# Half of a modulation sum moved to ScalarE and GpSimd, first down-projection copies to ScalarE, and two orderings changed in a one-core encoder step

## The chip, the cores and the metric

The kernel runs on 1 core of one Trainium2 chip. The metric is the device time of one execution in microseconds; lower is better. A core has a matrix engine (PE, TensorE), a vector engine (DVE, VectorE), an activation engine (ACT, ScalarE), a general engine (POOL, GpSimd) and a queue that issues DMAs (SP, SyncE). Each of them executes its own list of instructions strictly in order; an instruction whose semaphore is not yet set holds up everything behind it on that engine.

## The reference

One step of a one-layer streaming encoder over 1024 prompt frames and 32 sample frames, model width 1024, in f32:

```
mod = silu(c) @ w_mod + b_mod            # c: one row for the prompt, one for the sample
sh1, sc1, g1, sh2, sc2, g2, sh3, sc3, g3 = split(mod, 9)
h = rmsnorm(x, gains[0]) * (1 + sc1) + sh1
x = x + 0.5 * g1 * rmsnorm(swiglu(h, w1_gate, w1_up, w1_down), gains[1])     # block 1
h = rmsnorm(x, gains[2]) * (1 + sc2) + sh2
x = x + g2 * rmsnorm([GN(mixer A) ; GN(mixer B)] @ w_out, gains[3])          # mixers
h = rmsnorm(x, gains[4]) * (1 + sc3) + sh3
x = x + 0.5 * g3 * rmsnorm(swiglu(h, w2_gate, w2_up, w2_down), gains[5])     # block 2
swiglu(h, wg, wu, wd) = (silu(h @ wg) * (h @ wu)) @ wd                       # inner width 2816
```

`w_mod` is 1024 x 9216. Its product with the two rows of silu(c), one for the prompt and one for the sample, is what the code calls modulation.

## The kernel before

The 1056 frames are three token blocks `tb` = 0, 1, 2 of 384, 384 and 288 columns (the last holds the 32 sample frames); the features lie on the 128 partitions. Every f32 product is made from three matmuls: activation and weight are each split into a high part and a remainder, and high x high, high x low and low x high are summed in PSUM. A weight tile is split by `pair_of` (lines 539 and 540): ACT copies the high part, then DVE, or POOL for a sum of weights, subtracts to get the rest.

**The two feed-forward blocks** (`ffn`, key "h1" for block 1 and "h3" for block 2) run over 11 groups of 256 inner columns. A round is three stages: "g" (gate), "u" (up) and "d" (down). Gate and up of token blocks 0 and 1 are one Strassen-Winograd product (`strassen`): seven 12-matmul products instead of eight, from weights A11, A12, A21, A22 and their sums S1 to S4, which POOL adds (`Mat.of`, line 563) and splits (line 540), and from activation sums T1 to T4 (`combos`, lines 614 to 632). Token block 2 shares the weights A11 to A22. Round 0 uses no sums (`plain`), because T1 to T4 need the normed activations of both token blocks; its up weights lie in three places of a tile called `wu`. Before each product the code asks for the split of its own weight and of the next product's. In the down stage (`down`, lines 796 to 803) two PSUM banks `dn` fill; the first group of a token block copies them to the accumulator `facc` (line 801, DVE), later groups add them (line 803, DVE). `facc` of the attention output is called `fo`.

**Side work.** Norms, residuals, modulation and the sums T are Python generators in a list `side`; `step(n)` advances the first of them by n pieces, and calls of `step` stand between products. `begin` appends a generator (or puts it first), and `need(key)` runs the list until the one with that key is done. `between(F, tb, ...)` is residual and norm of one token block; its sums of squares go through a matmul with a column of ones (`pss`, line 374), a reciprocal root (`ry`, lines 351 to 355) and a broadcast (`pr`, line 422).

**Modulation.** The first 16 of 72 column blocks are made at the start by matmuls. The other 56 come as side work in block 1 (`mod_aside`, 19 chunks of up to 384 columns): a DMA brings 256 rows of `w_mod` into a tile `wma`, and for each of the eight 128-row slices DVE multiplies it by the silu column of the prompt (j = 0) and adds it to `macc` 0, and does the same for the sample (j = 1, `macc` 1): lines 248 (first slice) and 250. Then three transposes and a DVE reduction per row sum over the partitions (lines 256 and 257).

`wma`, the weight sums `ws` and the norms' scratch tiles share one pool of five buffers, "h". The order on each engine is not written by hand: a scheduler that lists the program's pieces by their place in the code, and by when it expects their inputs, sets it when the program is built. So a moved `begin` or a new request changes the lists of all engines.

Of the kernel before, what the change touches and what calls it, by code (L numbers as in the profile page):

```python
# [10 lines left out]
AF = mybir.ActivationFunctionType  # L11
OP = mybir.AluOpType
AX = mybir.AxisListType
# [68 lines left out]
def encoder_step(ctx: ExitStack, tc, x_prompt, x_sample, cache_a_k, cache_a_v, cache_b_k, cache_b_v,  # L82
# [152 lines left out]
    def mod_aside(c0, nc_):  # L235

        w = 128 * nc_
        acc = [s_tile([128, 384], "macc")[:, :w] for _ in range(2)]
        for g in range(4):
            r = h_tile([128, 2, 384], "wma")[:, :, :w]  # L240
            dma.dma_start(r, w_mod[0, 256 * g:256 * (g + 1), 128 * c0:128 * c0 + w]
                          .rearrange("(k p) n -> p k n", p=128))
            for kk in range(2):
                k = 2 * g + kk
                for j in range(2):
                    c = csil[:, k, j:j + 1]
                    if k == 0:
                        ve.tensor_scalar(acc[j], r[:, kk], c, None, op0=OP.mult)
                    else:
                        ve.scalar_tensor_tensor(acc[j], r[:, kk], c, acc[j], op0=OP.mult, op1=OP.add)  # L250
                yield
        yield
        for j in range(2):
            pt = pc("pmt", (128, 4, 128))
            for b in range(nc_):
                te.transpose(pt[:, b, :], acc[j][:, 128 * b:128 * b + 128], ident)
            ve.tensor_reduce(modT[:, j, c0:c0 + nc_], pt[:, :nc_, :], axis=AX.X, op=OP.add)
        coefs(c0, c0 + nc_)
        yield

# [390 lines left out]
    def ffn(key, H, tags, F, facc, wg, wu, wd, per_group, key_out, after, beside=lambda: None):  # L651
# [68 lines left out]
        def strassen(r, what, m, two, beside):  # L720
            w, w2 = 384, TB[2][1]
            B = {"B11": half(0, 0), "B21": half(0, 1), "B22": half(1, 1), **T}
            banks, v = {}, {}

            def bank(name):
                if name not in banks:
                    if name in "bd":
                        t = p2("gu")
                        banks["b"], banks["d"] = t[:, 0, :w], t[:, 1, :w]
                    elif name in "01":  # L730
                        t = p2("g2")
                        banks["0"], banks["1"] = t[:, 0, :w2], t[:, 1, :w2]
                    else:
                        banks[name] = p1("ge")[:, :w]
                return banks[name]

            def temp(name, f, tb):
                v[name] = s_tile([128, 384], "sl" if what == "g" else "ut")
                if what == "g":
                    sl[r, f, tb] = v[name]  # L740
                return v[name]

            def plus(out, b, x):
                ve.tensor_tensor(out, banks[b], v[x], op=OP.add)

            seq = [x for x in STRASSEN if two or x[1]]
            for n, (name, x, at, blk2) in enumerate(seq):
                w_ = m.split(name)
                if n + 1 < len(seq):
                    m.split(seq[n + 1][0])  # L750
                if x:
                    product(bank(at), w_, B[x], name in ("A11", "S2", "S1", "A22"), True)
                if two and blk2:
                    f, d = int(name[1]) - 1, int(name[2]) - 1
                    product(bank(str(f)), w_, half(2, d), name in ("A11", "A22"), True)
                beside(n)
                if name == "A11":
                    ae.activation(temp("s", 1, 0), banks["a"], AF.Copy)
                elif name == "A12":
                    made(r, what, 0, 0, banks["a"])  # L760
                elif name == "S2":
                    plus(temp("u", 0, 1), "b", "s")
                elif name == "S3":
                    plus(v["s"], "b", "s")
                    plus(temp("c", 1, 1), "d", "s")
                    made(r, what, 1, 1, v["c"])
                elif name == "A22":
                    plus(v["s"], "e", "s")
                    made(r, what, 1, 0, v["s"])
                elif name == "S4":  # L770
                    plus(v["u"], "d", "u")
                    made(r, what, 0, 1, v["u"])
                elif name == "A21":
                    made(r, what, 0, 2, banks["0"])
                    made(r, what, 1, 2, banks["1"])
                step(pace)
# [3 lines left out]
        def down(r, tb, m, mp):  # L780
            w = TB[tb][1]
            if mp == 0:
                owns[tb] = tb not in begun
                begun.add(tb)
                if owns[tb]:
                    F[tb] = facc(tb)
                if r == final[tb]:
                    if key_out != "y" or tb == 1:
                        finish()
                    owns[tb, "own"] = marked((key_out, tb), after(tb))  # L790
            ps = p2("dn")
            for s in range(2):
                k = 2 * mp + s
                for q in range(2):
                    g, (h, l) = gs[r, q, tb], m.w[q, k // 4]
                    te.matmul(ps[:, s, :w], h[:, k % 4, :], g[:, 0, :w], start=q == 0, stop=False)  # L796
                    te.matmul(ps[:, s, :w], h[:, k % 4, :], g[:, 1, :w], start=False, stop=False)  # L797
                    te.matmul(ps[:, s, :w], l[:, k % 4, :], g[:, 0, :w], start=False, stop=q == 1)  # L798
            o = F[tb][:, 2 * mp:2 * mp + 2, :]
            if owns[tb]:  # L800
                ve.tensor_copy(o, ps[:, :, :w])  # L801
            else:
                ve.tensor_tensor(o, ps[:, :, :w], o, op=OP.add)  # L803
            if r == final[tb]:
                next(owns[tb, "own"])
            step(1)
            if r == final[tb] and mp == KT // 2 - 1:
                side.append(owns[tb, "own"])
# [2 lines left out]
        yield  # L811
        load(1)
        yield
        for i, (r, what) in enumerate(stages):
            gi, blocks = plan[r]
            if (r, what) == (0, "u"):
                continue
            load(i)
            m = loaded[r, what]

            def nexts(n, last, i=i):
                if n == 0:
                    load(i + 1)
                elif n == last:
                    ready(i + 1)

            if what == "d":
                for q in range(2):
                    m.split(q, 0)
                order = list(blocks)  # L830
                ending = any(r == final[tb] for tb in order)
                todo = [(tb, mp) for tb in order for mp in range(4)] if ending else \
                    [(tb, mp) for h in range(2) for tb in order for mp in (2 * h, 2 * h + 1)]
                for n, (tb, mp) in enumerate(todo):
                    if n == 1:
                        for q in range(2):
                            m.split(q, 1)
                    down(r, tb, m, mp)
                    nexts(n, len(todo) - 3)
            elif r == 0:  # L840
                mu = loaded[r, "u"]
                mu.places = [(None, p) for p in wide(tags)] + [("r",)]
                for tb in blocks:
                    need((key, tb))
                    if tb == 1:
                        begin((key, "T"), combos(H, T, tags), first=key == "h3")
                    last = tb == blocks[-1]
                    plain(r, "g", m, tb, lambda n: None)
                    plain(r, "u", mu, tb, lambda n, last=last: nexts(n, 2, i + 1) if last else None)
            elif blocks == (2,):  # L850
                need((key, 2))
                plain(r, what, m, 2, lambda n: nexts(n, 2))
            else:
                need((key, "T"))
                if 2 in blocks:
                    need((key, 2))
                strassen(r, what, m, 2 in blocks, lambda n: nexts(n, 4 if what == "g" else 5))
            if what == "u" or r == 0 and what == "g":
                if 2 in blocks:
                    per_group(gi)  # L860
                if gi == NF // 2 - 1:
                    beside()
# [676 lines left out]
    while outs:  # L1539
        out_piece()  # L1540
        step(OUTSTEP)
    begin(("h3", 2), between(F2[2], 2, 1, H3))


    F3 = [None] * 3

# [80 lines left out]
```

## Time and profile before

| what | value |
|---|---|
| median of 3 runs | 2287.52 us (2286.5 to 2291.86) |
| the profiled execution | 2285.75 us, of which 2284.0 us are the span from first to last instruction |
| PE busy | 2118.2 us, 93% of the span |
| DVE, ACT, POOL busy | 1510.4 us (66%), 848.1 us (37%), 649.0 us (28%) |
| granted TensorE clock, mean | 0.969 |
| HBM traffic | 164.12 MB read, 22.86 MB written |

The profile lists instructions by source line. In its rows "x" is a count, then come the busy time in us and the mean ns of one, and after a bar the idle time of the engine in front of them with what ended it. A row of waits reads: who waited for whom, us in total, times, the longest. Block 1 runs from about 45 to 850 us, the projections and mixers to about 1470, block 2 from there to the end.

### The profile page before, as it was taken

What the parts mean: (1) busy time and instruction counts of PE and PEld (TensorE: products, weight loads), DVE (VectorE), ACT (ScalarE), POOL (GpSimd) and SP (SyncE); (2) the same over time, 40 slices, a digit from 0 to 9 for tenths busy, and PEclk for the clock granted to TensorE, in tenths of its full rate; (3) what the DMA queues carried; (4) which work ended last, traced back from release to release, by engine and by line L of the source; (5) the groups of instructions that cost most, each with busy time, mean ns of one, the idle gap of its engine ahead of it and who ended that gap; (6) DMA issues with size and microseconds to landing.
All of it is one profiled execution on the core that took longest, in us unless ns stands there. A gap on an engine that the chain in (4) does not pass through costs nothing.

```text
span 2284.0 us, 34644 instructions
## 1 busy us (share of the span) xinstructions
PE 2118.2 (93%) x13532; PEld 2003.9 (88%) x13532; DVE 1510.4 (66%) x2917; ACT 848.1 (37%) x1814; POOL 649.0 (28%) x609
## 2 busy tenths in 40 slices
PE   7888989999999998999999899967999999999998
PEld 4888989999999997889888578867999999999997
DVE  5888779888865687677544775677645455544548
ACT  4422212222223344467544673433332222332224
POOL 2333222333245212200100322335143323333311
PEclk8999999999999998999999899988999999999999
DMA  8133224333232254110210211421321111111123
GB/s 317 59 105 113 90 78 122 111 98 94 77 121 66 74 185 130 63 41 25 66 30 25 81 40 44 153 74 37 111 65 47 56 38 56 56 52 32 47 65 116
DMA packets 150842, 186.10 MB, mean 81 GB/s; under 512 B 7981, under 2 KB 134357, under 8 KB 149525
## 3 DMA queue, kind: packets, MB, share of 16 engines
q1 hardware_dynamic: 150676, 183.87, 26.0%
q8 instruction: 107, 1.75, 0.3%
q14 instruction: 59, 0.48, 0.1%
HBM read 164.12 MB, written 22.86 MB: 82 GB/s over the span
## 4 chain that ended last, share of the span: by engine, by line
PE 69%; DVE 16%; DMA 6%; POOL 4%; issue 2%; ACT 2%; SPq 0%; DVEq 0%; POOLq 0%; ACTq 0%
PE gu L598 9%; PE ge L598 8%; PE dn L796 6%; PE dn L797 6%; PE dn L798 6%; PE g L598 6%; DVE macc L250 5%; PE gate L598 3%; PE po L979 2%; POOL ws L563 2%; PE S L1018 2%; PE pq L342 2%; PE up L598 2%; DMA raw<-in_w_up_dram 2%; PE pq L344 2%
## 5 line engine op out<-in xcount | busy, mean ns | idle before, releaser
L796 PE MATMUL dn<-gg,w 128*128 128x384 f32 (+1 forms) x1008 | 333.2, 331 | 51.8 <-DVE facc L801 31.3
L540 POOL TENSOR_TENSOR w<-ws,w 128x512 fp32r<-128x512 f32 x160 | 220.9, 1388 | 550.7 <-ACT w L539 547.4
L540 DVE TENSOR_TENSOR w<-raw,w 128x512 fp32r<-128x512 f32 x298 | 240.2, 815 | 193.2 <-ACT w L539 192.3
L539 ACT ACTIVATE w<-raw 128x512 fp32r<-128x512 f32 x298 | 184.1, 629 | 474.6 <-PE dn L798 187.4
L797 PE MATMUL dn<-gg,w 128*128 128x384 f32 (+1 forms) x1008 | 327.6, 325 | 0.0
L798 PE MATMUL dn<-gg,w 128*128 128x384 f32 (+1 forms) x1008 | 327.5, 325 | 0.0
L803 DVE TENSOR_TENSOR facc<-dn,facc 128x768 f32<-128x768 f32 (+1 forms) x240 | 212.6, 887 | 156.1 <-PE dn L798 154.6
L598 PE MATMUL gu<-t,w 128*128 128x384 f32 x1440 | 264.5, 335 | 3.4 <-DVE facc L803 2.6
L598 PEld LDWEIGHTS gu<-t,w 128*128 128x128 f32 x1440 | 248.4, 188 | 4.4 <-issue 3.1
L796 PEld LDWEIGHTS dn<-gg,w 128*128 128x128 f32 x1008 | 191.7, 190 | 60.2 <-DVE facc L801 32.4
L598 PE MATMUL g<-h_hi,w 128*128 128x288 f32 x1024 | 224.1, 296 | 5.0 <-DVE w L540 2.3
L563 POOL TENSOR_TENSOR ws<-raw 128x512 f32<-128x512 f32 x80 | 116.5, 1456 | 308.3 <-DVE macc L250 109.7
L250 DVE SCALAR_TENSOR_TENSOR macc<-wma,csil,macc 128x384 f32<-128x384 f32 (+1 forms) x266 | 183.6, 728 | 17.2 <-DMA wma<-in_w_mod_dram 17.1
L797 PEld LDWEIGHTS dn<-gg,w 128*128 128x128 f32 x1008 | 191.7, 190 | 0.0
L798 PEld LDWEIGHTS dn<-gg,w 128*128 128x128 f32 x1008 | 191.3, 190 | 0.0
L598 PE MATMUL ge<-h,w 128*128 128x384 f32 x960 | 185.7, 336 | 0.4 <-ACT w L539 0.4
L598 PEld LDWEIGHTS g<-h_hi,w 128*128 128x128 f32 x1024 | 171.4, 188 | 7.8 <-DVE w L540 4.7
L539 ACT ACTIVATE w<-ws 128x512 fp32r<-128x512 f32 x160 | 99.2, 630 | 201.5 <-PE g L598 82.2
L598 PEld LDWEIGHTS ge<-h,w 128*128 128x128 f32 x960 | 166.6, 188 | 0.8 <-ACT w L539 0.6
L598 PE MATMUL g<-h_lo,w 128*128 128x288 f32 x512 | 151.2, 295 | 0.0
L698 ACT ACTIVATE gg<-sl 128x384 fp32r<-128x384 f32 (+1 forms) x132 | 61.7, 492 | 144.9 <-DVE sl L697 144.3
L598 PE MATMUL ge<-t,w 128*128 128x384 f32 x480 | 99.0, 343 | 12.5 <-DVE w L540 8.7
(294 smaller groups left out, 4374.8 us busy)
## 6 DMA issues: line engine op xcount, KB each, us to landing
raw<-in_w_gate_dram SPq DMA_DIRECT2D x54, 512.0 KB, 3.8
raw<-in_w_up_dram SPq DMA_DIRECT2D x54, 512.0 KB, 3.8
raw<-in_w_down_dram SPq DMA_DIRECT2D x54, 512.0 KB, 3.9
wma<-in_w_mod_dram SPq DMA_DIRECT2D x72, 384.0 KB, 3.4
raw<-in_w_in_dram SPq DMA_DIRECT2D x18, 512.0 KB, 4.0
raw<-in_w_out_dram SPq DMA_DIRECT2D x13, 512.0 KB, 5.2
wm<-in_w_mod_dram SPq DMA_DIRECT2D x8, 768.0 KB, 8.9
xr<-xs SPq DMA_DIRECT2D x16, 384.0 KB, 3.9
```

The source lines that it names most:

```text
L250: ve.scalar_tensor_tensor(acc[j], r[:, kk], c, acc[j], op0=OP.mult, op1=OP.add)
L342: te.matmul(ps, w[:, 0, k], hi, start=start, stop=False)
L344: te.matmul(ps, w[:, 1, k], hi, start=False, stop=stop)
L539: ae.activation(w[:, 0], src, AF.Copy)
L540: (by or ve).tensor_tensor(w[:, 1], src, w[:, 0], op=OP.subtract)
L563: (ge if name in SUMS_POOL else ve).tensor_tensor(a[name], x, y, op=op)
L598: te.matmul(ps, w[a][:, k, :], x[b][k], start=first and k == 0 and q == 0, stop=last and k == n - 1 and q == 2, skip_group_check=True)
L698: ae.activation(g[:, 0, :w], v, AF.Copy)
L796: te.matmul(ps[:, s, :w], h[:, k % 4, :], g[:, 0, :w], start=q == 0, stop=False)
L797: te.matmul(ps[:, s, :w], h[:, k % 4, :], g[:, 1, :w], start=False, stop=False)
L798: te.matmul(ps[:, s, :w], l[:, k % 4, :], g[:, 0, :w], start=False, stop=q == 1)
L803: ve.tensor_tensor(o, ps[:, :, :w], o, op=OP.add)
```

## The change

- `mod_aside`: the prompt row stays on DVE. For the sample row ACT multiplies each slice by its silu column into a new tile `wmn` of the pool "h", and POOL adds the two halves of `wmn` to each other and the sum to `macc` 1. The sums over the partitions become matmuls with a column of ones (stationary `macc`, one column moving) into a PSUM tile `pms`, and one DVE copy takes both rows out. The generator yields once more per chunk.
- `strassen`: a product asks for the splits of the next two weights instead of one.
- `down`: the first group's copy to `facc` is made by ACT instead of DVE.
- `ffn` for block 2: the sums T are put on the list right after norms of token blocks 0 and 1, and the norm of token block 2 (`between(F2[2], ...)`) behind them; before, that norm was begun first, and the sums were put in front of it when token block 1's turn came.

```
--- before.py
+++ after.py
@@ mod_aside
+            n = h_tile([128, 2, 384], "wmn")[:, :, :w]
             for kk in range(2):
                 k = 2 * g + kk
-                for j in range(2):
-                    c = csil[:, k, j:j + 1]
-                    if k == 0:
-                        ve.tensor_scalar(acc[j], r[:, kk], c, None, op0=OP.mult)
-                    else:
-                        ve.scalar_tensor_tensor(acc[j], r[:, kk], c, acc[j], op0=OP.mult, op1=OP.add)
+                if k == 0:
+                    ve.tensor_scalar(acc[0], r[:, kk], csil[:, k, 0:1], None, op0=OP.mult)
+                else:
+                    ve.scalar_tensor_tensor(acc[0], r[:, kk], csil[:, k, 0:1], acc[0], op0=OP.mult, op1=OP.add)
+                ae.activation(n[:, kk], r[:, kk], AF.Copy, scale=csil[:, k, 1:2])
+                if kk:
+                    to = acc[1] if g == 0 else n[:, 0]
+                    ge.tensor_tensor(to, n[:, 0], n[:, 1], op=OP.add)
+                    if g:
+                        ge.tensor_tensor(acc[1], acc[1], n[:, 0], op=OP.add)
                 yield
         yield
+        yield
+        pm = pc("pms")[:, :2 * nc_].rearrange("p (j b) -> p j b", j=2)
         for j in range(2):
-            pt = pc("pmt", (128, 4, 128))
             for b in range(nc_):
-                te.transpose(pt[:, b, :], acc[j][:, 128 * b:128 * b + 128], ident)
-            ve.tensor_reduce(modT[:, j, c0:c0 + nc_], pt[:, :nc_, :], axis=AX.X, op=OP.add)
+                te.matmul(pm[:, j, b:b + 1], acc[j][:, 128 * b:128 * b + 128], ones, start=j == 0 and b == 0,
+                          stop=j == 1 and b == nc_ - 1, skip_group_check=True)
+        ve.tensor_copy(modT[:, :, c0:c0 + nc_], pm)
         coefs(c0, c0 + nc_)
@@ strassen
                 w_ = m.split(name)
-                if n + 1 < len(seq):
-                    m.split(seq[n + 1][0])
+                for nx in seq[n + 1:n + 3]:
+                    m.split(nx[0])
@@ down
             if owns[tb]:
-                ve.tensor_copy(o, ps[:, :, :w])
+                ae.activation(o, ps[:, :, :w], AF.Copy)
@@ ffn
         load(1)
         yield
+        if key == "h3":
+            begin((key, "T"), combos(H, T, tags))
+            begin((key, 2), between(F2[2], 2, 1, H3))
@@ ffn, round 0
-                    if tb == 1:
-                        begin((key, "T"), combos(H, T, tags), first=key == "h3")
+                    if tb == 1 and key == "h1":
+                        begin((key, "T"), combos(H, T, tags))
@@ before block 2
-    begin(("h3", 2), between(F2[2], 2, 1, H3))
```

Line numbers of the changed kernel are 7 to 10 higher from `mod_aside` on (540 becomes 547, 563 becomes 570, 598 becomes 605).

The built programs show where instructions moved. **POOL in block 1**, early in the rounds; `ws` are the weight sums, `w` their splits. Before:

```order
L563 TENSOR_TENSOR ws<-ws,raw 128x512
L563 TENSOR_TENSOR ws<-raw,ws 128x512
L563 TENSOR_TENSOR ws<-raw 128x512
L540 TENSOR_TENSOR w<-ws,w 128x512 x3
L563 TENSOR_TENSOR ws<-raw 128x512
```

The changed kernel, in the same rounds:

```order
L253 TENSOR_TENSOR macc<-wmn 128x384
L570 TENSOR_TENSOR ws<-raw 128x512
L255 TENSOR_TENSOR macc<-macc,wmn 128x384
L570 TENSOR_TENSOR ws<-ws,raw 128x512
L547 TENSOR_TENSOR w<-ws,w 128x512
L570 TENSOR_TENSOR ws<-raw,ws 128x512
L253 TENSOR_TENSOR wmn<-wmn 128x384
L255 TENSOR_TENSOR macc<-macc,wmn 128x384
L547 TENSOR_TENSOR w<-ws,w 128x512
```

One or two modulation adds now stand in front of nearly every weight sum and split of POOL; there are 133 of them in the whole list.

**PE and DVE at the start of block 2.** PE before, from the gate product of token block 0 on:

```order
L598 MATMUL gate<-h,w 128x384 x13
L598 MATMUL up<-h,wu 128x384 x22
L422 MATMUL pr<-ident,ry 128x128 x3
L598 MATMUL up<-h,wu 128x384 x14
L598 MATMUL up<-h,w 128x384 x12
L598 MATMUL gate<-h,w 128x384 x32
```

PE of the changed kernel:

```order
L605 MATMUL gate<-h,w 128x384 x13
L429 MATMUL pr<-ident,ry 128x128 x3
L605 MATMUL up<-h,wu 128x384 x4
L605 MATMUL gate<-h,w 128x384 x18
L605 MATMUL up<-h,wu 128x384 x32
L605 MATMUL up<-h,w 128x384 x12
```

The broadcast `pr` of token block 1's norm comes before the up product instead of inside it, and of that product four matmuls stand in front of token block 1's gate. DVE before, at the same place (`sq` are sums of squares, `rv` the start of the reciprocal root):

```order
L492 TENSOR_TENSOR fo<-fo,xr 128x768 x2
L540 TENSOR_TENSOR w<-raw,w 128x512
L385 TENSOR_TENSOR sq<-sq 128x384
L540 TENSOR_TENSOR w<-raw,w 128x512 x3
L385 TENSOR_TENSOR sq<-sq 128x384
L540 TENSOR_TENSOR wu<-raw,wu 128x512
L387 TENSOR_TENSOR sq<-sq 128x384
L540 TENSOR_TENSOR wu<-raw,wu 128x512 x2
```

DVE of the changed kernel, from the norm of token block 1 on (`z` and `t_...` are the sums T):

```order
L452 SCALAR_TENSOR_TENSOR n<-fo,acoef,pr 128x384 x8
L478 SCALAR_TENSOR_TENSOR h<-n,modT,h 128x384 x6
L621 TENSOR_TENSOR z<-h 128x768 x3
L630 TENSOR_TENSOR z<-z 128x768
L633 TENSOR_TENSOR z<-z 128x768
L628 TENSOR_TENSOR t_14933<-z,t_14933 128x768
L636 TENSOR_TENSOR z<-z 128x768
L628 TENSOR_TENSOR t_14934<-z,t_14934 128x768
L639 TENSOR_TENSOR z<-z 128x768
L628 TENSOR_TENSOR t_14935<-z,t_14935 128x768
L547 TENSOR_TENSOR wu<-raw,wu 128x512
```

The splits of the up weights `wu` stood ahead of that norm; now the whole norm and most of the first half of the sums T stand ahead of them.

**The first `facc` copies of block 2.** Before, on DVE, between the sums T that follow token block 2's norm:

```order
L626 TENSOR_TENSOR z<-z 128x768
L621 TENSOR_TENSOR t_15055<-z,t_15055 128x768
L629 TENSOR_TENSOR z<-z 128x768
L621 TENSOR_TENSOR t_15056<-z,t_15056 128x768
L632 TENSOR_TENSOR z<-z 128x768
L801 COPY facc<-dn 128x768 x2
L621 TENSOR_TENSOR t_15057<-z,t_15057 128x768
```

In the changed kernel, on ACT, ahead of token block 2's norm (`h_hi`):

```order
L705 ACTIVATE gg<-sl 128x384
L808 ACTIVATE facc<-dn 128x768
L388 ACTIVATE sq<-fo 128x2x288
L808 ACTIVATE facc<-dn 128x768 x2
L546 ACTIVATE w<-raw 128x512
L808 ACTIVATE facc<-dn 128x768
L546 ACTIVATE w<-raw 128x512
L808 ACTIVATE facc<-dn 128x768
L765 ACTIVATE sl<-ge 128x384
L808 ACTIVATE facc<-dn 128x768
L476 ACTIVATE h_hi<-n,modT 128x256
```

Six of the eight copies have moved from behind that norm to ahead of it. In the rounds of block 2 after round 1 the lists of DVE, ACT and POOL are the same as before, and that of PE but for two rows, up to the last round.

## The prediction

> **What bounds the kernel now.** I read the busy time by stretches first. In its rows stand the stretch in us, its length, busy us and count of PE, PEld, DVE, ACT and POOL, the granted clock, the DMA share and GB/s: here most of block 1, the start of block 2, and block 2's steady rounds.
>
> ```profile
> 100.00:690.00 590.00, 537.22 (x3286) 524.69 (x3285) 478.17 (x787) 148.78 (x273) 194.06 (x133) 0.98 0.33 99
> 1470.00:1600.00 130.00, 95.32 (x516) 93.11 (x517) 95.11 (x180) 51.94 (x97) 51.51 (x38) 0.84 0.23 76
> 1600.00:2220.00 620.00, 611.35 (x3853) 606.42 (x3853) 312.35 (x437) 178.94 (x331) 198.84 (x143) 1.00 0.19 56
> ```
>
> Block 2's rounds leave PE idle for 8.65 us in 620. The same rounds in block 1, with modulation beside them, leave 52.8 in 590, and there DVE is busy for 81% of the time against 50%. At block 2's start 34.7 of 130 us are idle. Only these two stretches have anything to give. Next the waits of PE, first in block 1:
>
> ```profile
> PE dn L796 <- DVE facc L803: 12.1, 12, 2.5
> PE ge L598 <- DVE w L540: 7.9, 4, 2.8
> PE dn L796 <- DVE facc L801: 7.4, 2, 6.2
> PE dn L796 <- DVE sl L744: 5.1, 4, 1.8
> PE gu L598 <- DVE ut L744: 4.4, 1, 4.4
> PE ge L598 <- ACT w L539: 3.7, 2, 3.3
> PE dn L796 <- ACT sl L693: 2.6, 2, 1.3
> PE gu L598 <- DVE facc L803: 2.6, 1, 2.6
> PE gu L598 <- DVE sl L744: 1.8, 2, 1.1
> ...
> PE gu L598 <- POOL w L540: 1.0, 1, 1.0
> ```
>
> DVE's rows make 44.8 us (41.3 shown; four rows of 1.6 and less left out), ACT's 6.8, POOL's 1.0. PE waits here because DVE's list is full. In block 2's rounds, and at block 2's start (last three rows), it reads:
>
> ```profile
> PE gu L598 <- POOL w L540: 7.5, 9, 1.7
> PE g L598 <- DVE w L540: 0.7, 3, 0.3
> ...
> PE dn L796 <- DVE facc L801: 23.9, 2, 20.5
> ...
> PE pss L374 <- POOL sq L387: 4.3, 1, 4.3
> PE pr L422 <- DVE ry L355: 2.4, 1, 2.4
> ```
>
> Where DVE is at 50%, PE hardly waits for it, and the splits of the weight sums on POOL come late instead, a little. Block 2's start has 30.6 us of waits, one of 20.5.
>
> **Block 1: DVE.** The groups of the stretch 100 to 690 us; then the times of lines 250 and 1573 in the whole run (ns least, median, most), and the group of the `facc` copies:
>
> ```profile
> L250 DVE SCALAR_TENSOR_TENSOR macc<-wma,csil,macc 128x384 f32<-128x384 f32 x252 | 175.1, 733 | 17.1 <-DMA wma<-in_w_mod_dram 17.1
> L540 DVE TENSOR_TENSOR w<-raw,w 128x512 fp32r<-128x512 f32 x94 | 73.8, 791 | 27.0 <-ACT w L539 26.8
> L540 POOL TENSOR_TENSOR w<-ws,w 128x512 fp32r<-128x512 f32 x63 | 89.4, 1425 | 221.2 <-ACT w L539 217.9 <-DVE ut L744 3.1
> L563 POOL TENSOR_TENSOR ws<-raw 128x512 f32<-128x512 f32 x34 | 49.6, 1458 | 136.4 <-DVE macc L250 109.7 <-DMA raw<-in_w_up_dram 15.7 <-DMA raw<-in_w_gate_dram 4.4
> L257 DVE TENSOR_REDUCE modT<-pmt 128x3 f32<-128x384 f32 x36 | 19.7, 547 | 10.6 <-PE pmt L256 10.6
> L248 DVE TENSOR_SCALAR macc<-wma,csil 128x384 f32<-128x384 f32 x36 | 16.6, 497 | 0.0
> ...
> L250 DVE SCALAR_TENSOR_TENSOR macc<-wma,csil,macc x266: 467/606/1720, 124.0 to 610.5; 128x384 f32<-128x384 f32 x126, 128x256 f32<-128x256 f32 x7
> L1573 DVE TENSOR_SCALAR facc<-facc,gcoef x16: 227/411/1271, 2235.9 to 2269.2; 128x384 f32<-128x384 f32 x8, 128x256 f32<-128x256 f32 x4, 128x32 f32<-128x32 f32 x4
> ...
> L801 DVE COPY facc<-dn 128x768 f32<-128x768 f32 (+1 forms) x24 | 20.9, 880 | 4.6 <-PE dn L798 4.6
> ```
>
> The sample row takes half of line 250 and half of line 248 off DVE: 19 chunks x 7 = 133 by 0.733 us, 97.5, and 19 by 0.497, 9.4. The 38 reductions go, 38 by 0.547, 20.8; 19 copies of a few columns come for them at about the 0.227 that line 1573 takes for its 32 columns, 4. That is 124 off. POOL then runs more beside DVE: line 250's mean stands 127 ns over its median and 266 over its least while POOL is busy 33% of the time. POOL's share rises by 24 points (next part), so an operation with two inputs in SBUF, of which some 250 stay (126 of line 250, 94 of line 540, about 30 gating products), grows by 127 x 24/33 = 92 ns or, by the least, 193: 23 to 48 us. I take 23, since the 467 includes the shorter tiles. With the 12 `facc` copies of block 1 that go to ACT, by 0.88, 11, DVE falls by 124 + 11 - 23 = 112 us, to 62% of the stretch (366 of 590). Between 50%, with 0.7 us of waits, and 81%, with 44.8, a straight line gives 18 us at 62%. A wait falls faster than the load that causes it, so I take 12: **-33 us**, between -27 and -44.
>
> **Block 1: POOL, ACT, PE.** A POOL add of this size and an ACT scale, by the nearest rows (whole run), with two of PE's small sums:
>
> ```profile
> L385 POOL TENSOR_TENSOR sq<-sq 128x384 f32<-128x384 f32 (+1 forms) x48 | 49.9, 1049 | 189.1 <-ACT sq L381 166.5 <-PE S L1018 7.7 <-PE po L979 6.1
> L758 ACT ACTIVATE ut<-ge 128x384 f32<-128x384 f32 x20 | 9.8, 490 | 97.7 <-PE ge L598 97.7
> 495.25 0.49 PE L256 MATMUL pmt<-ident,macc 128*128 128x128 f32 x3
> 1479.67 0.72 PE L374 MATMUL pss<-ones,sq 128*128 128x1 f32 x6
> ```
>
> POOL gets 133 adds by 1.05 us, 140 us: from 33% to 57%. They stand in front of nearly every weight sum and split, and a split of a sum is what PE waits for in block 2. At 33% there it costs 7.5 us; with the adds I put 10 here for the 1.0 of now, **+9**. The bounds are 0 (63 splits, all with slack) and 132 (each of the 63 behind two adds, 2.1 us, no slack); I stay near the low one because POOL sat idle for 221 us in front of these splits, waiting for ACT. ACT gets 152 scales by 0.49, 74 us, and the copies, some 9: from 25% to 39%. Block 2's rounds have it at 29% and show no wait for it, so the 6.8 become about 11, **+4** (0 to 10). PE's sums change from twice three transposes per chunk (0.98 us by this row) to six matmuls with ones (0.72): 19 x 0.26 = 5 less at best, and 0 where they fill an idle moment, which I take. Each chunk has 11 yields for 10, so the modulation, whose line 250 runs from 124.0 to 610.5, lasts a tenth, 49 us, longer. Nothing needs it before the block's end at 690 or later, so it is hidden; for its load in the last round I set **+3** (0 to 5). The DMAs stay as they are; but `wmn` takes turns in the five buffers with `wma` and `ws`. That `ws` waits 109.7 us for line 250 shows that buffers are short; on PE this is inside the +9. Fewer waits give clock back: 0.98 against 1.00 over 590 us is 12 lost, of which I take **-4**. Block 1: -33 + 9 + 4 + 3 - 4 = **-21**, from +10 to -50.
>
> The trace has a call of line 1573 (median 411 ns) on DVE that a POOL operation overlaps:
>
> ```profile
> 2251.26 1.27 DVE L1573 TENSOR_SCALAR facc<-facc,gcoef 128x384 f32<-128x384 f32 x1
> 2251.30 1.01 POOL L385 TENSOR_TENSOR sq<-sq 128x384 f32<-128x384 f32 x1 [2.32 <-ACT sq L381]
> ```
>
> The Trainium skill's "SBUF — State Buffer", section "SBUF: two separate sides", says that GpSimd and VectorE share one pair of ports as an exclusive lock, held for a whole instruction, against which a VectorE operation with two SBUF inputs fully blocks. The 1.27 against 0.411 agrees. By that rule every add costs DVE up to its own length, which is the second rival below; by line 250's mean it costs a part of it.
>
> **Block 2's start.** The present order in time, DVE and PE, from the middle of round 0:
>
> ```profile
> 1484.63 0.16 DVE L355 SCALAR_TENSOR_TENSOR ry<-rt,ry 128x3 f32<-128x3 f32 x1
> 1488.64 0.83 PE L422 MATMUL pr<-ident,ry 128*128 128x128 f32 x6
> 1489.51 4.29 DVE L445 SCALAR_TENSOR_TENSOR n<-fo,acoef,pr 128x384 f32<-128x384 f32 x8 [4.72 <-PE pr L422]
> 1494.18 2.31 DVE L471 SCALAR_TENSOR_TENSOR h<-n,modT,h 128x384 fp32r<-128x384 f32 x4
> 1534.62 2.45 POOL L614 TENSOR_TENSOR z<-h 128x768 f32<-128x768 f32 x1 [0.69 <-DVE h_lo L471]
> 1547.25 0.94 DVE L632 TENSOR_TENSOR z<-z 128x768 f32<-128x768 f32 x1
> 1549.12 0.69 PE L796 MATMUL dn<-gg,w 128*128 128x384 f32 x1 [20.50 <-DVE facc L801]
> ```
>
> PE waits 20.5 us for copies that stand on DVE behind token block 2's norm and half of the sums T. With the copies on ACT, six of eight ahead of that norm, I leave 0.8 us of it (one copy), and the norm's `pss` and `pr` come while PE has rounds to do, so their 6.7 go too. What is late next is `wu`. `pr` can start when `ry` is there, 1484.9, 3.7 us sooner; then DVE runs n x8 (4.29) and h x6 (2.31 for four, some 4.3 with waits) to 1494.4, then, ahead of the first moved `wu` split, ten sums T by 0.94, 9.4, and one wait for POOL's z, 2.45: 1506.2. PE has only the end of `pr` at 1485.8, its up product standing behind that split: 20.4 us idle, less some 0.7 of matmuls: 19.7 (12 if DVE and POOL share the sums without waiting; 32 if five POOL sums by 2.45 all lie in line with DVE's). On ACT and POOL token block 2's norm now lies beside round 1; its first split of a sum comes some 3 us late. Waits: 19.7 + 0.8 + 3 = 23.5 for 30.6, -7; the clock of 0.84 over 95 busy us costs 15, and with a quarter less idle I take -2: **-9**, from +12 to -18.
>
> **The rest.** Splits asked two ahead leave the lists of block 2's steady rounds as they are: 0. In block 1 that order is in what was said of POOL. In block 2's tail a few rows trade places, 0 +- 1. The norms of the mixers are untouched.
>
> Sum: -21 - 9 = -30. The profiled execution has 2285.75 us (2284.0 of span), 1.8 under the median of 2287.52. 2285.75 - 30 + 1.8 = 2257.5: I say **2257**.
>
> **Rivals.**
> First (chance 0.12), more than forecast: all DVE waits go, POOL's and ACT's adds have slack, half of the clock's loss and more comes back (-50), and block 2's start comes to -18. 2287.5 - 68 = 2220. The 221 us of idle time before POOL's splits speak for it, the wait of 7.5 in block 2 at a POOL share of 32% against.
> Second (0.17): each add holds up DVE for its whole length. 133 x 1.05 = 140 us come for the 134 taken off, block 1 gains nothing, only block 2's start does: 2287.5 - 9 = 2278. The 1.27 us above speaks for it; line 250's median of 606, in a stretch where POOL is busy a third of the time, and that DVE operations reading PSUM need not meet it, against.
> Third, slower (0.16): POOL's queue. An add waits for two scaled slices, which wait on ACT for the DMA of `wma`; the splits of S1 to S4 stand behind them. A pair of adds is 2.1 us, and line 250's row has 17.1 us of waits for that DMA. If half of the 63 splits come 2 us late, +64 for my +9: 2257 + 55 = 2312. It decides from 9 + 30 = 39 us on, 0.62 us late for each of the 63. Against it: the request two ahead, and the idle time.
> Fourth (0.05): `wu` comes so late that block 2's start loses 12, block 1 as forecast: 2287.5 - 21 + 12 = 2278.
>
> My forecast has 0.50, with 2240 to 2272 as its own range. Over 0.3%, 6.9 us, is about what can be told from no change: faster holds the forecast, the first rival and some 0.10 of the second and fourth, which lie 9 us down; same the rest of these, 0.12; slower 0.16. The range 2232 to 2290 leaves out most of the third rival and about half of the first.
>
> **What will show it.** Right: PE's waits for DVE in block 1 fall from 44.8 to 10 to 20 us; PE's idle time in that stretch falls from 52.8 to about 30; no `dn` wait of 20 us after 1500, but one of about 20 before `up<-h,wu`. The second rival: line 250's mean goes far over 733 ns and DVE stays near 80%. The third: PE's waits for POOL's line 547 (540 before) over 40 us. I would be wrong most likely by the POOL term, of which the trace shows no case at 57%.

## The result, and the profile after

| | before | changed |
|---|---|---|
| median, us | 2287.01 (2285.95 to 2291.86, 4 runs) | 2305.98 (2300.64 to 2308.02, 4 runs) |
| profiled execution, its span | 2285.75, 2284.0 | 2300.64, 2298.9 |
| ratio to before, 95% interval | | 1.0075 [1.0053, 1.0097] |

Slower by 17 us (12 to 22), where 30 less were forecast. The profiled execution is the shortest of the four; the others are 5 to 7 us longer at a clock of 0.961 to 0.962 against its 0.966, so that much is not in the trace below.

The same matmul of block 1, the 1201st of the `dn` product, stands in the two timelines (before, then changed) at:

```profile
722.02 0.33 PE L796 MATMUL dn<-gg,w 128*128 128x384 f32 x1
...
734.24 0.33 PE L803 MATMUL dn<-gg,w 128*128 128x384 f32 x1
```

So 12.2 of the trace's 15 us are lost in block 1. The busy times of the changed kernel, in stretches that end at the same work as the prediction's three (690, 1470 to 1600, 1600 to 2220):

```profile
100.00:702.20 602.20, 556.61 (x3394) 541.75 (x3393) 424.76 (x603) 230.49 (x436) 347.96 (x266) 0.97 0.32 97
1483.50:1615.60 132.10, 97.20 (x516) 93.36 (x517) 92.41 (x172) 58.24 (x105) 54.17 (x38) 0.84 0.23 74
1615.60:2235.60 620.00, 612.35 (x3854) 608.01 (x3853) 306.02 (x433) 180.30 (x336) 199.01 (x143) 1.00 0.19 56
```

In block 1 PE's idle time fell, 52.8 to 45.6 us, and PE's busy time rose, 537.2 to 556.6. DVE's busy time fell from 478.2 to 424.8, to 71% of the stretch where 62% was forecast. The steady rounds of block 2 kept their time to 0.1 us. Block 2's start lost 2.1, and the part between the blocks 1.3. The waits of PE in block 1 (and one of ACT in the whole run):

```profile
PE ge L605 <- ACT w L546: 16.4, 8, 3.5
PE dn L803 <- DVE facc L810: 10.3, 12, 1.7
PE dn L803 <- ACT facc L808: 4.5, 3, 2.3
PE ge L605 <- DVE w L547: 2.9, 5, 1.8
...
PE gu L605 <- POOL w L547: 1.4, 1, 1.4
...
ACT wmn L250 <- DMA wma<-in_w_mod_dram: 97.9, 41, 8.2
```

With the rows not shown, waits for DVE went from 44.8 to 22.5 us, those for ACT from 6.8 to 21.4, those for POOL from 1.0 to 1.4. The new sums, in the timeline of the changed kernel and in the group by source line:

```profile
L262 PE MATMUL pms<-ones,macc x224: 164/250/353, 133.1 to 675.2; 128*128 128x1 f32 x112
...
141.19 0.72 PE L262 MATMUL pms<-ones,macc 128*128 128x1 f32 x6
141.78 0.38 PE L803 MATMUL dn<-gg,w 128*128 128x288 f32 x1
```

112 sums are 224 records: each of these f32 products with one column runs in two passes. The next matmul starts 0.59 us after the first of three sums, here as at the median of the 18 such groups at full clock. Three transposes took 0.25 (before, from 495.25 to the next matmul, at 495.50):

```profile
495.50 0.60 PE L598 MATMUL ge<-h,w 128*128 128x384 f32 x2
```

38 groups by 0.34 make 13 us more of PE. Block 1 then reads: +13 for the sums, +5 of clock (the clock records show 10.2 us lost before and 15.4 after, to the same matmul), -7 of idle time: 11 of the 12.

### The profile page after: what moved, and what is told of

The parts are those of the page before. It is cut to its first block, busy times and chain, and to the rows that moved or that the text cites. A ratio compares the mean times of both kernels' runs of the same rounds, so it can differ in the third digit from the quotient of the medians.

```text
span 2298.9 us, 35045 instructions
## 1 busy us (share of the span) xinstructions
PE 2140.8 (93%) x13644; PEld 2023.3 (88%) x13644; DVE 1449.5 (63%) x2722; ACT 939.0 (41%) x1990; POOL 810.0 (35%) x742
## 4 chain that ended last, share of the span: by engine, by line
PE 54%; DVE 7%; POOL 4%; DMA 3%; ACT 2%; issue 2%; DVEq 0%; SPq 0%; POOLq 0%; ACTq 0%
PE gu L605 6%; PE ge L605 6%; PE dn L804 4%; PE dn L803 4%; PE dn L805 4%; PE g L605 4%; PE po L989 3%; POOL ws L570 2%; PE S L1028 2%; PE pq L349 2%; PE pq L351 2%; PE pq L350 2%; PE gate L605 2%; DMA raw<-in_w_up_dram 2%; PE pp L1052 1%
## 5 line engine op out<-in xcount | busy, mean ns | idle before, releaser
L547 DVE TENSOR_TENSOR w<-raw,w 128x512 fp32r<-128x512 f32 x298 | 257.2, 871 | 237.6 <-ACT w L546 229.2
L249 DVE SCALAR_TENSOR_TENSOR macc<-wma,csil,macc 128x384 f32<-128x384 f32 (+1 forms) x133 | 123.6, 929 | 30.5 <-DMA wma<-in_w_mod_dram 29.0
L250 ACT ACTIVATE wmn<-wma,csil 128x384 f32<-128x384 f32 (+1 forms) x152 | 84.7, 602 | 117.7 <-DMA wma<-in_w_mod_dram 97.9
L605 PE MATMUL ge<-t,w 128*128 128x384 f32 x480 | 107.2, 362 | 23.1 <-ACT w L546 19.1
```

The lines of the kernel that those rows point to most:

```text
L249: ve.scalar_tensor_tensor(acc[0], r[:, kk], csil[:, k, 0:1], acc[0], op0=OP.mult, op1=OP.add)
L250: ae.activation(n[:, kk], r[:, kk], AF.Copy, scale=csil[:, k, 1:2])
L547: (by or ve).tensor_tensor(w[:, 1], src, w[:, 0], op=OP.subtract)
L605: te.matmul(ps, w[a][:, k, :], x[b][k], start=first and k == 0 and q == 0, stop=last and k == n - 1 and q == 2, skip_group_check=True)
```

## The experiments

Ratios are to the kernel before, run beside each; the us beside them are for 2288 us.

### One part at a time

e1 is `mod_aside` as in the diff, e2 the `down` part, e3 the `ffn` part (the moved `begin` calls), e4 the `strassen` part, each alone.

> The kernel before with the modulation part alone (sample row over ACT and POOL, sums over the partitions by matmuls with ones, one yield more). Theory A, the loss is in block 1 and is the modulation's: PE pays some 13 us for the two-pass sums with ones, waits for ACT rise by about 15 us, waits for DVE fall by about 20, the clock costs some 5: 2287 + 13 = 2300, between 2295 and 2308. Rival B, the loss is the order at block 2's start or comes from the splits: modulation alone keeps the relief of DVE, 2287 - 10 = 2277. The page should show waits of PE for ACT's weight copies of 10 us and more in block 1 under A.

> The kernel before with the first facc copies on ACT alone. Theory A: the waits of dn for DVE's line 801 go, 7.4 us in block 1 and some 20 of the 23.9 at block 2's start: 2287 - 25 = 2262, between 2258 and 2272. Rival B: what PE does not wait for there it waits for right behind it, since token block 2's norm and the sums T still stand in DVE's list before round 1's sums can be used: 2287 - 7 = 2280.

> The kernel before with the sums T ahead of token block 2's norm in block 2 alone (facc copies on DVE). Theory A, it trades one wait of 20 us (dn for facc) for another of 20 (up product for wu): 2287 +- 4, with the wait for wu in the trace. Rival B, it is the loss of the changed kernel: 2287 + 12 to 20 = 2299 to 2307. Rival C, it gains as forecast: 2278.

> The kernel before with splits asked two products ahead alone. Theory A: the lists of the steady rounds hardly change, 2287 +- 3. Rival B: in block 1 the earlier request puts copies of later weights on ACT and subtractions on DVE ahead of work that PE needs sooner, 2287 + 8 = 2295 or more.

| | median, us | ratio [95%] | us |
|---|---|---|---|
| e1 modulation | 2311.88 | 1.0099 [1.0081, 1.0116] | +23 |
| e2 `facc` copies on ACT | 2278.35 | 0.9957 [0.9942, 0.9972] | -10 |
| e3 sums T first | 2293.07 | 1.0014 [1.0004, 1.0024] | +3 |
| e4 splits two ahead | 2294.18 | 1.0020 [1.0010, 1.0031] | +5 |

The sum is 21, the whole change measured 17 (12 to 22): the loss is the modulation, and more than theory A gave it. Up to that matmul of block 1, e1's trace has 12.6 us less of waits for DVE, 8.3 more for ACT and 20.5 more lost to the clock, where theory A had 20, 15 and 5. e2 fell between its two theories, since at block 2's start its wait only changed engine:

```profile
PE dn L796 <- ACT facc L801: 19.5, 1, 19.5
...
1547.36 0.84 ACT L620 ACTIVATE t<-z 128x768 fp32r<-128x768 f32 x1 [0.90 <-DVE z L629]
1548.11 1.49 ACT L801 ACTIVATE facc<-dn 128x768 f32<-128x768 f32 x2
```

The copies stand in ACT's list behind cuts of T (line 620) that wait for DVE's sums. e3 traded that wait for one of the same length, as theory A said: `up<-h,wu` for ACT's line 539, 19.6 us. e4 is a small loss, not the nothing of theory A: block 1 took 4 us longer in its trace, with 4 us less of idle time and 8.6 us more lost to the clock.

### Inside the modulation

e5 puts only the sums with ones into the kernel before (and the yield); e6 only the row on ACT and POOL:

```
e5:  mod_aside before, from "yield" on as in the change (pms, matmuls with ones, one copy)
e6:  mod_aside of the change, from "yield" on as before (pmt, transposes, reductions)
```

> The kernel before with one thing changed: the partition sums of macc by matmuls with ones into pms and one copy, in place of transposes and reductions; both rows still on DVE. Theory A: PE pays 38 groups of 0.59 us for 38 of 0.25, 13 us, some more half-clock stretches behind these one-column matmuls, 3 us, and DVE's 18 us less give back some 5: 11 us over the kernel before, 6 to 18. Rival B: the sums are free on PE and only DVE's relief counts: 3 to 5 us under it.

> The kernel before with the sample row moved to ACT and POOL, but the partition sums by transposes and DVE reductions as before (and no added yield). Theory A: of the 22 us that the whole modulation part cost, 13 were the sums with ones and some more its clock; the row alone costs 5 us over the kernel before, 0 to 10, with waits of PE for ACT of over 12 us in block 1. Rival B: the row's move is a gain that the sums hid: 8 us or more under it. Rival C: the row alone makes the loss: 15 to 22 over it.

e5: 2288.06 us, 1.0004 [0.9993, 1.0015]. e6: 2291.35 us, 1.0015 [1.0004, 1.0027], +3. So e5 missed both of its theories; both parts together lose 23 where apart they lose 4. To see why, the sample row was taken away altogether (e9; both sums then from the prompt row), and the sums with ones put on top of that (e10):

```
e9, e10:
-                for j in range(2):
+                for j in range(1):
```

> The kernel before with the sample row's 152 DVE multiplications left out (its two sums are then taken from the prompt row), nothing put on ACT or POOL. It gives the relief of DVE by itself. Theory A, the prediction's step: PE's waits for DVE come from DVE's load, and with some 107 us less of it they fall from 44.8 to about 12: 30 us under the kernel before, 25 to 40. Theory B: these waits are the latency of chains (weight copy on ACT, subtraction on DVE, matmul) and of the order in the lists, which a shorter list hardly shortens: 5 to 12 us under it, with over 25 us of waits for DVE left.

> As the one without the sample row, with the partition sums by matmuls with ones. Beside the kernel before these sums cost 1 us. Theory A: they cost PE 13 us always, and beside a full DVE list the 18 us that they take off DVE pay for it; without the sample row DVE has slack, and they cost 10 to 15 us over the kernel without the row. Theory B: their price does not depend on DVE's load: 0 to 3 us over it.

e9: 2256.14 us, 0.9856 [0.9834, 0.9878], **33 us under** the kernel before. e10: 2270.83 us, 0.9920 [0.9898, 0.9941]: the sums with ones cost 15 us there and 1 us in e5. PE pays the 13 us for the passes in both, and DVE is relieved in both. What the relief gives back is idle time of PE. From 100 us up to the 1201st `dn` matmul the traces read (lost to the clock is time multiplied by the share of the clock that was not granted):

| | matmul at, us | PE idle, us | lost to the clock, us |
|---|---|---|---|
| before | 722.0 | 53.0 | 10.2 |
| e5, sums | 725.3 | 41.2 | 13.7 |
| e6, row | 730.8 | 53.9 | 13.7 |
| e1, both | 749.0 | 49.1 | 30.7 |
| e9, no row | 690.2 | 28.0 | 5.1 |
| e10, no row, sums | 703.8 | 25.6 | 8.5 |

The sums take 11.8 us of idle time off PE in e5, but 2.4 from e9 to e10, where DVE has slack, and 4.8 from e6 to e1. In the traces they so cost 15 us more on top of e6 than alone (18.3 against 3.3). 7 of these are idle time that is not won back. The other 8 are busy time of PE, in traces that count 17.0 us of lost clock from e6 to e1 against 3.5 in e5; why the clock is lost there is open. The waits of PE in e9, to the same place in block 1 (690 us), and its row of line 250:

```profile
PE dn L796 <- DVE facc L803: 11.0, 7, 2.3
PE dn L796 <- DVE facc L801: 6.2, 1, 6.2
PE pmt L256 <- DVE macc L250: 3.7, 3, 1.5
PE gu L598 <- POOL w L540: 1.6, 2, 1.4
...
L250 DVE SCALAR_TENSOR_TENSOR macc<-wma,csil,macc 128x384 f32<-128x384 f32 x126 | 95.4, 759 | 15.5 <-DMA wma<-in_w_mod_dram 13.8
```

Waits for DVE fall to 25 us, none of them long but one, and the time by 33: the time is theory A's, the waits that are left are theory B's. Waits for ACT fall from 6.8 to 0.5 as well, and the lost clock by 5. So DVE's relief is worth 33, and in e6 ACT and POOL give all of it back. Which of them, e13 (ACT's scales without POOL's adds) and e14 (POOL's adds on the unscaled slices, without ACT) ask. Their edits, against e6 (both sums of e13 come from the prompt row):

```
e13:
-                    ge.tensor_tensor(to, n[:, 0], n[:, 1], op=OP.add)
-                    if g:
-                        ge.tensor_tensor(acc[1], acc[1], n[:, 0], op=OP.add)
e14:
-                ae.activation(n[:, kk], r[:, kk], AF.Copy, scale=csil[:, k, 1:2])
-                    ge.tensor_tensor(to, n[:, 0], n[:, 1], op=OP.add)
+                    ge.tensor_tensor(to, r[:, 0], r[:, 1], op=OP.add)
```

> The sample row's ACT scales alone: the kernel before with DVE's half of the row left out, the 152 scaled slices written to wmn by ACT, POOL's 133 adds left out (both sums from the prompt row). DVE's relief alone gave 33 us; with ACT and POOL at work 3 us were lost, so 36 are given back. Theory A, ACT's list gives most of them back (scales that wait for wma hold the weight copies behind them): this kernel is only 5 to 15 us under the kernel before, with over 10 us of PE's waits for ACT. Theory B, POOL does: it stays 27 to 33 us under it.

> POOL's 133 adds alone: DVE's half of the row and ACT's scales left out, POOL adds the unscaled slices of wma. Theory A (ACT's list): 25 to 33 us under the kernel before. Theory B, POOL's adds give the gain back, by holding up DVE's operations at the ports they share and by standing ahead of the splits of weight sums: 3 to 12 us under it, with line 250's mean (761 ns without the row, 901 with it on both) at 850 ns or more. Theory C, each gives back about half: both this and the ACT kernel lie 12 to 22 us under it.

e13: 2271.97 us, 0.9935 [0.9917, 0.9952], -15: ACT's scales give 18 of the 33 back, but not as theory A said: PE's waits for ACT are 4.8 us there, not 10 and more. Both kernels also bring `wmn` into the five buffers of the pool "h", and no run separates that from the engines' work. e14: 2302.53 us, 1.0070 [1.0057, 1.0083], +16: POOL's adds give back 49, more than any theory had. Line 249 (250 before) in e13, e6 and e14, and three rows of e14's timeline:

```profile
L249 DVE SCALAR_TENSOR_TENSOR macc<-wma,csil,macc 128x384 f32<-128x384 f32 x126 | 100.5, 799 | 28.0 <-DMA wma<-in_w_mod_dram 26.5
...
L249 DVE SCALAR_TENSOR_TENSOR macc<-wma,csil,macc 128x384 f32<-128x384 f32 x126 | 115.1, 913 | 35.5 <-DMA wma<-in_w_mod_dram 34.1
...
L249 DVE SCALAR_TENSOR_TENSOR macc<-wma,csil,macc 128x384 f32<-128x384 f32 x126 | 130.0, 1032 | 18.0 <-DMA wma<-in_w_mod_dram 16.8
...
303.73 0.61 DVE L249 SCALAR_TENSOR_TENSOR macc<-wma,csil,macc 128x384 f32<-128x384 f32 x1
305.28 1.34 POOL L254 TENSOR_TENSOR macc<-macc,wmn 128x384 f32<-128x384 f32 x1
305.68 1.36 DVE L249 SCALAR_TENSOR_TENSOR macc<-wma,csil,macc 128x384 f32<-128x384 f32 x1
```

The call at 303.73 meets no POOL operation and takes 0.61 us. The one at 305.68 starts while POOL runs; POOL ends at 306.62 and the call at 307.04, 0.42 later. That is the rule: of the calls that start beside a POOL operation and meet no other, the median ends 415 to 418 ns after POOL's end in each kernel of the table below. The Trainium skill's "SBUF — State Buffer", section "SBUF: two separate sides", has such a rule: the port pair of the two engines is held for a whole instruction and the other blocks. The trace agrees. A call that waits takes 1.2 to 1.4 us on average, one that does not 0.61. A call that starts 64 ns or more ahead of POOL's operation is not held up: all 17 of the changed kernel take 0.60 to 0.62. With a lead of 7 to 44 ns (six calls, in e1, e9, e13 and e14) it waits as well. What differs between kernels is how many of the 128x384 calls start while POOL runs:

| | calls that start beside a running POOL operation | us against before |
|---|---|---|
| before | 44 of 252 | 0 |
| the whole change | 68 of 126 | +17 |
| e9, no row | 26 of 126 | -33 |
| e13, ACT alone | 30 of 126 | -15 |
| e6, ACT and POOL | 63 of 126 | +3 |
| e14, POOL alone | 84 of 126 | +16 |
| e11, DMA ahead (below) | 80 of 126 | +22 |

The counts go with POOL's adds; the 18 us between e9 and e13 are not in them. What the adds cost is seen best from e9 to e14, up to the same matmul:

```profile
100.00:690.19 590.19, 562.24 (x3469) 551.12 (x3468) 422.63 (x661) 159.83 (x294) 202.55 (x143) 0.99 0.34 103
100.00:740.79 640.79, 582.09 (x3469) 565.82 (x3469) 485.70 (x661) 159.42 (x294) 365.39 (x276) 0.96 0.31 95
```

DVE runs 661 operations in both and is busy 63 us longer in e14. PE's idle time rises by 31 us (its waits for DVE from 25.2 to 49.8) and its busy time by 20, with 19 us more lost to the clock.

In e14 an add and a multiplication are released by the same DMA, so they meet most often; in e6 the add comes later, after ACT's scale. That this is why e14 loses more than e6 is argued from these counts, not shown apart. POOL's own queue costs little: PE's waits for POOL's splits are 1.4 us in e14 and in e6.

ACT's part was tried by issuing each `wma` DMA one pair of slices earlier, with the row on ACT and POOL (e11), and in e2's kernel with both rows on DVE (e12):

```
e11, e12:
-            r = h_tile([128, 2, 384], "wma")[:, :, :w]
-            dma.dma_start(r, ...)
+            r = ahead.pop(0)[:, :, :w]
+            ahead.append(fetch(c0, nc_, g + 1) if g < 3 else fetch(c0 + 3, min(3, 69 - c0), 0))
```

> The sample row on ACT and POOL with transposes, with each DMA of wma issued one pair of slices ahead of its use. Without that it cost 3 us over the kernel before. Theory A: ACT's scales wait for wma and hold the weight copies behind them; ahead of time the DMA has landed, ACT's waits for wma fall from about 100 us to under 30, PE's for ACT from 12 to under 6, and the kernel is 3 to 8 us under the kernel before. Theory B: buffers of the pool, not the DMA's latency, are what is late, and it stays at 0 to 5 us over it.

> The kernel before with the first facc copies on ACT, and each DMA of wma issued one pair of slices ahead of its use (both rows on DVE). Theory A: the 17 us that DVE waits for wma go, and some 4 us of PE's waits with them: 13 us under the kernel before, 11 to 16. Theory B: as the facc copies alone, 8 to 10 us under it, or less, if the buffer held longer delays the weight sums.

e11: 2312.57 us, 1.0096 [1.0077, 1.0114], +22. Its mechanism came as theory A said, its time did not. Waits of ACT for `wma` in e6, then in e11, and PE's waits for ACT's weight copies in both:

```profile
ACT wmn L250 <- DMA wma<-in_w_mod_dram: 116.0, 44, 8.8
PE ge L603 <- ACT w L544: 11.3, 7, 2.5
...
ACT wmn L261 <- DMA wma<-in_w_mod_dram: 10.1, 7, 3.4
PE gu L614 <- ACT w L555: 2.8, 2, 2.1
PE ge L614 <- ACT w L555: 1.2, 2, 0.7
```

So the wait for the DMA does hold up weight copies on ACT. But with it gone more calls of DVE meet POOL (63 to 80 of 126), and waits of PE for DVE rose from 39.3 to 58.6 us, one kind of them (`pmt` for `macc`) from 4.8 to 13.7. That the meetings cause this is not shown: `wma` also holds its buffer longer, and ACT's weight copies wait 36.1 us for POOL's `ws`, against 5.7 in e6. e12: 2277.24 us, 0.9940 [0.9922, 0.9959], -14, the time of theory A: DVE's waits for `wma` fall from 17.1 to 3.6 us. It has the lowest time of these kernels that compute the whole step, under both the kernel before and the changed one. Its interval overlaps that of e2, so a gain over e2 is not shown.

### Block 2's start

e7 is e2 and e3 together; e8 adds an early request for the up weights:

```
e8:
                 for tb in blocks:
                     need((key, tb))
+                    if tb == blocks[0] and key == "h3":
+                        for name in ("A11", "A12", "A21"):
+                            mu.split(name)
```

> The kernel before with the first facc copies on ACT and the sums T ahead of token block 2's norm, nothing else. Theory A: the two add up, -10 and +3: 7 us under the kernel before, 3 to 10, with a wait of 19.6 us for wu at block 2's start. Rival B: each wait of 20 us was there only because of the other, and both go: 20 us under it.

> As the one with facc copies on ACT and the sums T first, and block 2's round 0 asks for the first three splits of the up weights (wu) right after token block 0's norm, so that they stand ahead of token block 1's norm on ACT and DVE. Theory A: the 19.6 us wait for wu was head-of-line only; it falls under 6 us, and the kernel is 15 to 20 us under the kernel before. Rival B: PE then waits the same time for the next thing, token block 1's normed activations or the sums T: 7 us under it.

e7: 2284.82 us, 0.9989 [0.9978, 1.0000], -3, with the wait for `wu` of 19.6 us: the low end of theory A. e8: 2278.94 us, 0.9962 [0.9949, 0.9976], -9. The waits at block 2's start in e8:

```profile
PE pss L374 <- POOL sq L387: 9.2, 1, 9.2
PE gu L598 <- ACT w L539: 8.2, 1, 8.2
PE gate L598 <- DVE w L540: 4.5, 1, 4.5
PE dn L796 <- ACT facc L801: 4.3, 1, 4.3
PE ge L598 <- ACT w L539: 3.8, 1, 3.8
PE pr L422 <- DVE ry L355: 3.3, 1, 3.3
```

The wait of 19.6 is gone, as theory A said, and the next things in line take its place: 33 us in six waits. Theory B is right about the time. Before, that stretch had 36 in waits, in e3 and e7 37. In the five orders tried (before, e2, e3, e7, e8) these waits make 32 to 37 us: mostly, the order decides which matmul waits for the two norms and the sums T. That the work itself sets this time is argued from these sums, not shown apart.

## Why the prediction was wrong

In block 1 the waits and rows above give -22 for DVE, +0.4 for POOL, +14.6 for ACT, +13 for the sums and +5 for the clock, 11 of the measured 12, where -21 was forecast.

**DVE's relief, -33: near in number, and partly by luck.** e9 measures 33 us for the row's relief alone. But the text let PE's waits for DVE fall to 12, the `facc` copies taken off too; in e9 they stop at 25, and ACT's waits and the clock make up the rest. In the changed kernel waits for DVE fell by 22.3, since DVE's load fell less than worked out.

**What POOL's adds do: the first step that failed.** The text priced them in POOL's queue, +9, where 0.4 is measured, and put their effect on DVE at 92 ns for each of some 250 operations, from the mean over the median. Line 249 measures 943 ns in the changed kernel against 759 in e9, 184 more and near the upper end named (193), and DVE's weight splits rose from 791 to 988 ns. So DVE's busy time fell by 53 us in that stretch, not by 112, and stayed at 71% of it. The mean was the wrong view: the calls have two durations, 0.61 and some 1.3 us, and the share that waits rose from 44 of 252 to 68 of 126. The second rival named this mechanism and gave block 1 no gain (2278); e6, with the row alone, ends at +3. Its sign, DVE near 80%, did not come: not every add costs DVE its whole length.

```profile
L249 DVE SCALAR_TENSOR_TENSOR macc<-wma,csil,macc 128x384 f32<-128x384 f32 x126 | 118.8, 943 | 30.2 <-DMA wma<-in_w_mod_dram 28.8
L547 DVE TENSOR_TENSOR w<-raw,w 128x512 fp32r<-128x512 f32 x94 | 92.5, 988 | 65.4 <-ACT w L546 57.6 <-DMA raw<-in_w_down_dram 4.6 <-POOL macc L255 2.9
```

**ACT, +4: mis-sized.** 14.6 us, outside the 0 to 10 given; 4.5 of them are waits for the `facc` copies that ACT now makes. ACT's load rose as worked out (to 38%), but the load was not the point: a scale that waits for `wma` holds the weight copies behind it, 97.9 us of waits in all, and PE's waits for these copies fall when the DMA comes earlier (e11). The text saw that wait only as a trouble of POOL. In e13 ACT waits as long for `wma`, 99 us, and PE only 4.8 for ACT, so the wait costs PE most beside POOL's adds; why is open.

**The sums with ones, 0 with bounds of -5 and 0: a misread row.** The `pss` row of 0.72 us "x6" was taken for six sums and is three sums in two passes; the three transposes were taken at the row's 0.49 us, and the next matmul starts after 0.25. The price is 13 us of PE, and 15 in e10.

**The clock, -4:** +5 in the trace: seven half-clock stretches between 110 and 860 us, five before. The +3 for the last round cannot be told apart; the sums ran to 675 us.

**Block 2's start, -9:** +2.1. The wait for `wu` was forecast at 19.7 us and came as 19.6:

```profile
PE up L605 <- ACT wu L546: 19.6, 1, 19.6
PE pss L381 <- POOL sq L394: 4.5, 1, 4.5
PE gate L605 <- DVE w L547: 4.5, 1, 4.5
PE gu L605 <- ACT w L546: 3.6, 1, 3.6
PE ge L605 <- ACT w L546: 2.7, 1, 2.7
```

Two steps failed. The first is "their 6.7 go too". The two waits meant, at token block 2's second sum of squares, did go, but another of 4.5 came at its first: PE's list holds that `pss` ahead of a gate product, and POOL's squares for it come late. The second is the 3 us for a late split: copies of weights on ACT came late by 6.3. The text also counted 30.6 us of waits before, in three rows; with the smaller ones left out there, 4.5 for `gate` above all, which stayed, they are 36, and 37 in the changed kernel. The idle time did not shrink, and the clock stayed at 0.84.

**The third rival** (slower, 2312) was nearest in time and wrong in cause: POOL's splits came 1.4 us late in all, not over 40. The splits two ahead, "0", cost 5 us alone, in block 1 (e4); the text looked at block 2's lists and left block 1 to POOL's term.

Open: 5 us of the median that the profiled execution does not show; how much of ACT's and POOL's price in e13 and e14 is the buffers that `wmn` takes; why ACT's 18 us (e13) and POOL's 49 (e14) give only 36 together; and of e1's 23 us, the 20 of lost clock in its trace (30.7 for 10.2 before), where four of twelve half-clock stretches follow a group of `pms` and the rest other waits.

## What to carry to other kernels

Work taken off the engine that others wait for was worth 33 us when it disappeared and nothing when it moved. Before work is moved to an engine that holds up the first, look at the two durations of the operations that meet, not at their mean, and at what releases both. Be careful with a scale or copy that waits for a DMA in a list that feeds the matmuls. A relief pays for a side cost only while the relieved engine is the bound, so two changes that each come out about even can lose together.

## What the runs showed of the hardware

- A DVE operation of line 249 or 250 that starts while a POOL operation runs ends, at the median, 415 to 418 ns after that one's end; alone, or when it starts 64 ns or more ahead, it takes 0.61 us.
- A one-column f32 matmul is two records: three sums over 128 partitions hold PE for 0.59 us, three 128x128 f32 transposes for 0.25.
- PE's half-clock stretches last 3.41 us or two or three times that (110 to 860 us of the traces of before, changed and e1), so each loses 1.7 us of clock or more; where idle time stood in front of one it was often only 1.2 to 2.5 us of the 3.6 before. The Trainium skill's "TensorE: Matmul & The Clock Gate", section "Part 1: The HAM clock gate (the "warmup" mystery)", gives half clock after an idle window of some 3.4 us: the length agrees, but here often less than a whole window of idle time stood before a stretch.
